# Down projection of a hybrid transformer block: form copies queued one piece later, results finished in the residual's tiles, fewer shared load buffers

## The chip, the cores and the metric

The kernel runs on one NeuronCore of one Trainium2 chip. The metric is the device time of one execution in microseconds; lower is better. The engines named below are TensorE (PE, with its weight loads as PEld), VectorE (DVE), ScalarE (ACT), GpSimd (POOL) and SyncE (SP). Each engine takes its instructions strictly in the order of its own program; SP, ACT and POOL also issue transfers.

## The reference

One transformer block over 256 tokens of width 2048: three kinds of attention merged by gates, an output projection added to the residual, then a gated feed-forward layer with a short causal convolution. Only its last lines matter here:

```python
h2 = rms_norm(x, g_ffn[l])
u = causal_depthwise_conv(h2 @ w_up[l], conv_w[l], conv_b[l])
u_gate, u_val = jnp.split(u, 2, axis=-1)
x = x + (jax.nn.silu(u_gate) * u_val) @ w_down[l]      # 256 x 5632 times 5632 x 2048
```

All tensors are float32. The changed part is the last line, called the down stage here.

## The kernel before, in words

**Number format.** A float32 product is done in three passes. Each operand is split into a rounded part `hi` (type fp32r) and the remainder `lo = x - hi`; `three` (lines 890 to 892) multiplies hi by hi, lo by hi and hi by lo into one PSUM bank. For a weight tile that is loaded into `raw`, `parts` makes `hi` by a cast on ACT (line 885) and `lo` by a subtraction on DVE (line 886). There are four `hi` and four `lo` tiles in rotation, so a cast may start only when PE has read the tile used four casts earlier.

**Pieces.** The 5632 rows of `w_down` are 44 tiles of 128 rows; two neighbours form a piece, 22 pieces in all. The output's 2048 columns are done in two halves (`nb` 0 and 1) of 1024. A piece is multiplied in one of two ways. `eight` is the plain way: eight blocks (two row tiles, two halves of the tokens, two blocks of 512 columns), 24 matmuls in two steps. `seven` does the same with seven products, as Strassen and Winograd do: 21 matmuls in four steps. It needs sums of the weights, two of which (`T`) were made during the stage before and are loaded as `raw_t`; the other two, the plain sums `t13`, are made here by DVE (lines 947 and 948) out of the two loaded tiles `raw_s`. It also needs sums of the activations, the forms. The trace leaves numbers out, so that both `hi_t42` (the split of the loaded `T`) and `hi_t13` (the split of the plain sums) read `hi_t` there.

**Forms.** `forms(p)` prepares piece `p`'s activations: five small DVE instructions (lines 855 to 859) that end in the tile `fr`, then two ACT copies of it to hi parts (lines 862 and 863, into `sf` and `aT`), and then two DVE subtractions for the lo parts (lines 865 and 866). It is a generator: each `yield` ends what is queued in one step, and the rest is queued a step later. There is one `fr` tile.

**Order.** Two strings, `PLANS`, say in which order the pieces come: `s` for seven, `e` for eight. The first half is eeee, eight times se, ee; the second is e, four times se, sse, three times se, ssee. Loads and splits are written two steps ahead of the matmuls that use them. Every instruction of the down stage that is wrapped in `keep` stays on its engine in the order written; PE's matmuls are ordered by the scheduler. A form set is queued with each `e` from the second on, eight sets in the first half and three in the second, so that most of them fall into a repeat of `s` and `e`.

**Load buffers.** `buffer(name)` gives the tiles for loads and for the plain sums: the first six from four tiles tagged `raw`, after that in turn from those and from four tiles tagged `more`. A load waits until its tile has been read by its last reader.

**Results.** `gather` adds the seven-product sums into the residual's tiles `xr`, which POOL loads (line 977). At the end of each half `results` adds the other PSUM banks: DVE writes `o` (line 1016), a tile of the two-tile pool `junk`, and ACT's queue sends it (line 1017). After the first half come one `e` and then the first `s` of the second half, so that these four sends stand in ACT's program ahead of that `s`'s first cast.

Of the kernel before, what the change touches and what calls it, by code (L numbers as in the profile page):

```python
# [9 lines left out]
F32 = mybir.dt.float32  # L10
F32R = mybir.dt.float32r
AF = mybir.ActivationFunctionType
ALU = mybir.AluOpType
AX = mybir.AxisListType

P = 128
# [16 lines left out]
PIECE = 1024  # L33
# [11 lines left out]
def hybrid_block(  # L45
# [25 lines left out]
    nc = tc.nc  # L71
# [5 lines left out]
    sm = ctx.enter_context(tc.tile_pool(name="sm", bufs=4))  # L77
# [742 lines left out]
    def down_pool():  # L820
        if not dn:
            uv.close()
            side.close()
            dn.append(ctx.enter_context(tc.tile_pool(name="dn", bufs=4, side="right", reuse_waits="tile")))
        return dn[0]

    keep = tc.keep_in_program_order
    ov = out[0].rearrange("(t p) d -> p t d", p=P)
# [3 lines left out]
    def pieces_at(p):  # L832
        return aT[:, 2 * p : 2 * p + 2]

    def pieces_of(p):
        return pieces_at(p).rearrange("p k (l t q) -> p k l t q", l=2, t=NT)

    def form_of(p, f):
        if f == FS4:
            return pieces_of(p)[:, 0, :, 1]  # L840
        if p < 10:
            return sf[:, p, f]
        return pieces_at(31 - p).rearrange("p k (f l q) -> p (k f) l q", f=2, l=2)[:, f]

    def forms(p):

        flat = aT[:, 2 * p : 2 * p + 3].rearrange("p k s -> p (k s)").bitcast(F32)
        v = flat[:, :1024].rearrange("p (k l t q) -> p k l t q", k=2, l=2, t=NT)
        d = sm.tile([P, 512], F32, tag="junk", bufs=2, name=f"fd_{p}").rearrange("p (f l q) -> p f l q", f=2, l=2)
        r = down_pool().tile([P, 512], F32, tag="fr", bufs=1, name=f"fr_{p}").rearrange("p (f q) -> p f q", f=4)  # L850
        g = rbc.rearrange("p (k q) -> p k q", k=2)
        two = flat[:, : 2 * 640].rearrange("p (a b) -> p a b", b=640)[:, :, :512]
        two = two.rearrange("p a (l t q) -> p a l t q", l=2, t=NT)[:, :, :, 0]
        tt = nc.vector.tensor_tensor
        keep(tt(d, two, v[:, 0, :, 1].unsqueeze(1).to_broadcast([P, 2, 2, P]), ALU.subtract))
        keep(tt(g, v[:, :, 0, 0], v[:, :, 1, 0], ALU.add))
        keep(tt(r[:, :2], d[:, :, 0], d[:, :, 1], ALU.add))
        keep(nc.vector.scalar_tensor_tensor(r[:, FS2], r[:, FS1], -1.0, g[:, 0], ALU.mult, ALU.subtract))
        keep(tt(r[:, FS4], r[:, FS2], g[:, 1], ALU.add))
        to = sf[:, p] if p < 10 else form_of(p, slice(0, 3))  # L860
        last = form_of(p, FS4)
        keep(nc.scalar.copy(to[:, :, 0], r[:, :3]))
        keep(nc.scalar.copy(last[:, 0], r[:, FS4]))
        yield
        keep(tt(to[:, :, 1], r[:, :3], to[:, :, 0].bitcast(F32), ALU.subtract))
        keep(tt(last[:, 1], r[:, FS4], last[:, 0].bitcast(F32), ALU.subtract))

    turn = [0]

    def buffer(name):  # L870
        turn[0] += 1
        if turn[0] > 6 and turn[0] % 2:
            return down_pool().tile([P, PIECE], F32, tag="more", name=name)
        return wp.tile([P, PIECE], F32, tag="raw", name=name)

    def load(src, name):
        raw = buffer(f"raw_{name}")
        keep(nc.sync.dma_start(raw, src))
        return raw

    def parts(src, name):
        n = src.shape[1]
        hi = wp.tile([P, PIECE], F32R, tag="hi", bufs=SBUFS, name=f"hi_{name}")
        lo = wp.tile([P, PIECE], F32R, tag="lo", bufs=SBUFS, name=f"lo_{name}")
        keep(nc.scalar.copy(hi[:, :n], src))  # L885
        keep(nc.vector.tensor_tensor(lo[:, :n], src, hi[:, :n].bitcast(F32), ALU.subtract))
        return [(hi[:, i : i + 512], lo[:, i : i + 512]) for i in range(0, n, 512)]

    def three(o, ah, al, w, first=False, last=False):
        nc.tensor.matmul(o, lhsT=ah, rhs=w[0], start=first, stop=False)  # L890
        nc.tensor.matmul(o, lhsT=al, rhs=w[0], start=False, stop=False)  # L891
        nc.tensor.matmul(o, lhsT=ah, rhs=w[1], start=False, stop=last)  # L892

    def a_of(k, t):
        a = aT[:, k]
        return a[:, t * P : (t + 1) * P], a[:, S + t * P : S + (t + 1) * P]

    def f_of(p, f):
        to = form_of(p, f)
        return to[:, 0], to[:, 1]  # L900
# [30 lines left out]
    def seven(p, n0, X, Y, first, last):  # L931
        k0, k1 = 2 * p, 2 * p + 1
        name = f"{n0}_{p}"
        w, raw = {}, {}

        def p0():
            raw[0] = load(dv[:, k0, n0 : n0 + PIECE], f"s{n0}_{k0}")
            (w["00"],) = parts(raw[0][:, :512], f"s{n0}_{k0}")

        def p1():  # L940
            raw[1] = load(dv[:, k1, n0 : n0 + PIECE], f"s{n0}_{k1}")
            w["10"], w["11"] = parts(raw[1], f"s{n0}_{k1}")

        def p2():
            raw[2] = load(made[n0 // PIECE, p], f"t{name}")
            raw[3] = buffer(f"t13_{name}")
            keep(nc.vector.tensor_tensor(raw[3][:, :512], raw[0][:, :512], raw[0][:, 512:], ALU.add))
            keep(nc.vector.tensor_tensor(raw[3][:, 512:], raw[0][:, 512:], raw[1][:, 512:], ALU.add))
            w["T4"], w["T2"] = parts(raw[2], f"t42_{name}")

        def p3():
            w["T1"], w["T3"] = parts(raw[3], f"t13_{name}")

        def u0():
            three(Y()[0], *a_of(k0, 0), w["00"], first, last)

        def u1():
            three(X()[0][0], *a_of(k1, 0), w["10"])
            three(X()[0][1], *f_of(p, FS4), w["11"])

        def u2():
            three(Y()[1], *f_of(p, FS2), w["T2"], first, last)
            three(X()[1][0], *a_of(k1, 1), w["T4"])

        def u3():
            three(Y()[2], *f_of(p, FS1), w["T1"], first, last)
            three(Y()[3], *f_of(p, FS3), w["T3"], first, last)

        steps.extend(((p0, u0), (p1, u1), (p2, u2), (p3, u3)))

    xrows = {}
# [25 lines left out]
    banks = {}  # L997
# [9 lines left out]
    def results(nb):  # L1007
        for t in range(NT):
            for n in range(2):
                o = sm.tile([P, 512], F32, tag="junk", bufs=2, name=f"o_{nb}_{t}_{n}")  # L1010
                parts_ = 2 if (nb, t, n) == (1, 1, 1) else 1
                for i in range(parts_):
                    w = 512 // parts_
                    oc = slice(i * w, (i + 1) * w)
                    xc = slice(nb * PIECE + n * 512 + i * w, nb * PIECE + n * 512 + (i + 1) * w)
                    keep(nc.vector.tensor_tensor(o[:, oc], xrows[nb, t, n][:, oc], banks[nb][0][t][n][:, oc], ALU.add))
                    nc.scalar.dma_start(ov[:, t, xc], o[:, oc])

    formed = 0
    after_step = {}  # L1020
# [4 lines left out]
    for nb, plan in enumerate(PLANS):  # L1025
        n0 = nb * PIECE
        ns, s = plan.count("s"), 0
        X, Y = (lambda nb=nb: banks[nb][0]), (lambda nb=nb: banks[nb][1])
        straight = list(range(FT // 2 - 1, ns - 1, -1)) if nb else list(range(ns, FT // 2))
        n_done = 0  # L1030
        at(len(steps) - 1, lambda nb=nb: start(nb))
        for i, c in enumerate(plan):
            if c == "s":
                seven(s, n0, X, Y, s == 0, s == ns - 1)
                s += 1
                if s == ns:
                    at(len(steps) - 1, lambda nb=nb: later(gather(nb, banks[nb][1])))
            else:
                eight(straight.pop(0), n0, X, i == 0, i == len(plan) - 1)
                n_done += 1  # L1040
                if n_done == 4:
                    at(len(steps) - 1, lambda nb=nb: residual(nb))
                if formed < ns and n_done >= 2:
                    at(len(steps) - 2, lambda p=formed: later(forms(p)))
                    formed += 1
        assert s == ns and not straight and formed >= ns
        at(len(steps) - 1, finish)
        at(len(steps) - 1, lambda nb=nb: results(nb))
# [44 lines left out]
```

## Time and profile before

| what | value |
|---|---|
| median of 3 runs | 1517.44 us (1516.77 to 1518.1) |
| the profiled execution: its time, its span | 1517.59 us, 1515.9 us |
| PE, DVE, ACT busy over the span | 98%, 69%, 57% |
| down stage, first to last matmul | 1256.79 to 1509.63 us of the span |

The span is the time from the first to the last instruction seen by the profiler; the execution's own time lies 1.69 us above it. "Busy" PE counts a matmul from its start to its modelled end, and successive matmuls overlap. A row of the timeline has its start, its duration, its engine and line, and in square brackets the idle time before it and what ended that. A row of waits has who waited for whom, the total, the count and the longest. A row of windows has the busy time and the number of instructions of each engine in one stretch, and PE's granted clock.

### The profile page before, as it was taken

The numbers are of one execution on the slowest core, as the hardware profiler recorded it, in microseconds if no ns is written. First come the engines' busy times: TensorE is split into PE (matmuls) and PEld (weight loads), VectorE is DVE, ScalarE is ACT, GpSimd is POOL, SyncE is SP. The second block draws the span as 40 slices with busy tenths as digits, with TensorE's granted clock in tenths as the row PEclk, the third lists the DMA queues.
The fourth block names the chain that finished last, engine by engine and source line by source line (L and its number), as shares of the span: only waits on it lengthen the run. The fifth ranks groups of instructions, "written<-read, shape, count | busy, mean of one in ns | idle before, by whom it ended". The sixth has DMA issues, their size and how long they took to land.

```text
span 1515.9 us, 20136 instructions
## 1 busy us (share of the span) xinstructions
PE 1489.3 (98%) x7408; PEld 1250.9 (83%) x7408; DVE 1044.5 (69%) x1333; ACT 859.6 (57%) x1225; POOL 33.6 (2%) x77
## 2 busy tenths in 40 slices
PE   9999999999999999999999999999999998899998
PEld 7888888888888888888888888888888886677786
DVE  5766566455655556565567877887787776886887
ACT  6755454368444444444566776776676675554553
POOL 0000000001000000000000000000000000000000
PEclk9999999999999999999999999999999999999999
DMA  8675475475667666666677778778777765677784
GB/s 302 193 206 158 128 220 154 126 215 152 197 201 207 191 204 196 191 194 196 210 222 260 254 251 289 237 257 277 250 252 269 250 184 191 208 253 243 226 288 142
DMA packets 156177, 327.70 MB, mean 216 GB/s; under 512 B 11290, under 2 KB 20142, under 8 KB 156078
## 3 DMA queue, kind: packets, MB, share of 16 engines
q1 hardware_dynamic: 150798, 310.15, 66.0%
q0 software_dynamic: 3952, 14.16, 2.6%
q10 hardware_dynamic: 1328, 2.11, 0.4%
q8 instruction: 58, 0.95, 0.3%
q14 instruction: 41, 0.34, 0.1%
HBM read 312.21 MB, written 14.16 MB: 215 GB/s over the span
## 4 chain that ended last, share of the span: by engine, by line
PE 92%; ACT 3%; DVE 2%; issue 1%; DMA 1%; POOL 0%; ACTq 0%; DVEq 0%; SPq 0%; POOLq 0%
PE u L805 22%; PE u L807 11%; PE g L158 5%; PE g L160 5%; PE g L159 5%; PE d L890 4%; PE d L892 4%; PE d L891 4%; PE s L158 2%; PE s L160 2%; PE s L159 2%; PE f L158 2%; PE f L160 2%; PE f L159 2%; PE b L158 2%; PE b L160 2%
## 5 line engine op out<-in xcount | busy, mean ns | idle before, releaser
L805 PE MATMUL u<-hT,hi_u 128*128 128x512 f32 x1408 | 442.4, 396 | 0.1
L807 PEld LDWEIGHTS u<-hT,lo_u 128*128 128x128 f32 x1408 | 264.5, 188 | 62.5
L807 PE MATMUL u<-hT,lo_u 128*128 128x256 f32 x1408 | 276.6, 278 | 0.0
L148 DVE TENSOR_TENSOR lo_u<-raw_u,hi_u 128x1024 fp32r<-128x1024 f32 x176 | 214.2, 1222 | 71.9 <-ACT hi_u L147 70.0
L147 ACT CAST hi_u<-raw_u 128x1024 fp32r<-128x1024 f32 x176 | 183.4, 1048 | 102.0 <-PE u L805 94.4
L805 PEld LDWEIGHTS u<-hT,hi_u 128*128 128x128 f32 x1408 | 214.3, 189 | 0.5 <-issue 0.5
L148 DVE TENSOR_TENSOR lo_g<-raw_g,hi_g 128x1024 fp32r<-128x1024 f32 x96 | 117.7, 1229 | 101.4 <-ACT hi_g L147 98.8
L147 ACT CAST hi_g<-raw_g 128x1024 fp32r<-128x1024 f32 x96 | 100.8, 1052 | 121.8 <-PE g L159 96.9
L158 PE MATMUL g<-hi_g,xT 128*128 128x512 f32 x384 | 150.9, 393 | 0.0
L160 PE MATMUL g<-lo_g,xT 128*128 128x512 f32 x384 | 149.6, 390 | 0.0
L159 PE MATMUL g<-hi_g,xT 128*128 128x512 f32 x384 | 149.5, 389 | 0.0
L160 PEld LDWEIGHTS g<-lo_g,xT 128*128 128x128 f32 x384 | 72.1, 188 | 15.3
L159 PEld LDWEIGHTS g<-hi_g,xT 128*128 128x128 f32 x384 | 72.2, 188 | 14.6
L158 PEld LDWEIGHTS g<-hi_g,xT 128*128 128x128 f32 x384 | 72.1, 188 | 14.5
L890 PE MATMUL d<-hi_d,aT 128*128 128x512 f32 x200 | 79.2, 396 | 4.3 <-ACT hi_d L885 4.3
L744 DVE TENSOR_TENSOR y<-y,z 128x512 f32<-128x512 f32 x88 | 60.8, 691 | 26.9 <-ACT z L743 23.1
L892 PE MATMUL d<-lo_d,aT 128*128 128x512 f32 x200 | 78.7, 394 | 0.0
L891 PE MATMUL d<-hi_d,aT 128*128 128x512 f32 x200 | 78.6, 393 | 0.0
L743 ACT ACTIVATE z<-u,taps 128x256 f32<-128x256 f32 x176 | 74.6, 496 | 0.0
L148 DVE TENSOR_TENSOR lo_s<-raw_s,hi_s 128x1024 fp32r<-128x1024 f32 (+1 forms) x40 | 44.7, 1118 | 37.1 <-ACT hi_s L147 37.1
L148 DVE TENSOR_TENSOR lo_f<-raw_f,hi_f 128x1024 fp32r<-128x1024 f32 (+1 forms) x40 | 44.7, 1119 | 34.5 <-ACT hi_f L147 33.0
L147 ACT CAST hi_f<-raw_f 128x1024 fp32r<-128x1024 f32 (+1 forms) x40 | 38.6, 967 | 52.3 <-PE f L159 47.6
(323 smaller groups left out, 2801.4 us busy)
## 6 DMA issues: line engine op xcount, KB each, us to landing
raw_u<-in_w_up_dram SPq DMA_DIRECT2D x176, 512.0 KB, 4.6
raw_g<-in_w_in_dram SPq DMA_DIRECT2D x96, 512.0 KB, 4.0
raw_d<-in_w_down_dram SPq DMA_DIRECT2D x50, 512.0 KB, 5.6
r<-in_w_down_dram SPq DMA_DIRECT2D x76, 256.0 KB, 5.7
raw_s<-in_w_down_dram SPq DMA_DIRECT2D x38, 512.0 KB, 6.3
raw_f<-in_w_in_dram SPq DMA_DIRECT2D x32, 512.0 KB, 3.7
raw_s<-in_w_in_dram SPq DMA_DIRECT2D x32, 512.0 KB, 3.7
raw_o<-in_w_out_dram SPq DMA_DIRECT2D x32, 512.0 KB, 4.9
```

The source lines that it names most:

```text
L147: pin(nc.scalar.copy(hi[:, :m], raw[:, :m]))
L148: pin(nc.vector.tensor_tensor(lo[:, :m], raw[:, :m], hi[:, :m].bitcast(F32), ALU.subtract))
L158: nc.tensor.matmul(o, lhsT=xh, rhs=wh, start=first, stop=False)
L159: nc.tensor.matmul(o, lhsT=xl, rhs=wh, start=False, stop=False)
L160: nc.tensor.matmul(o, lhsT=xh, rhs=wl, start=False, stop=last)
L743: nc.scalar.activation(z[:, i], u[:, i, j : j + S], AF.Copy, scale=taps_of(j, i))
L744: nc.vector.tensor_tensor(y, y, z, ALU.add)
L805: nc.tensor.matmul(ps, lhsT=hi[:, j, c], rhs=hT[:, k + j, :], start=first, stop=False)
L807: nc.tensor.matmul(ps[:, :S], lhsT=lo[:, j, c], rhs=hT[:, k + j, :S], start=False, stop=last)
L890: nc.tensor.matmul(o, lhsT=ah, rhs=w[0], start=first, stop=False)
L891: nc.tensor.matmul(o, lhsT=al, rhs=w[0], start=False, stop=False)
L892: nc.tensor.matmul(o, lhsT=ah, rhs=w[1], start=False, stop=last)
```

## The change

`forms` gets a second `yield`: the two ACT copies are queued one step after the five DVE instructions, the two subtractions one step after the copies. The plain sums have two tiles of their own (tag `t13`), and loads have six tiles: four `raw` and two `more`, of which every third load takes one. `results` adds in place into `xr` and sends `xr`; the first half's sends go out on POOL's queue, the second's still on ACT's.

```diff
@@ forms
         keep(tt(r[:, FS4], r[:, FS2], g[:, 1], ALU.add))
+        yield
         to = sf[:, p] if p < 10 else form_of(p, slice(0, 3))
@@ buffer
-        if turn[0] > 6 and turn[0] % 2:
-            return down_pool().tile([P, PIECE], F32, tag="more", name=name)
+        if turn[0] > 8 and turn[0] % 3 == 0:
+            return down_pool().tile([P, PIECE], F32, tag="more", bufs=2, name=name)
@@ seven, p2
-            raw[3] = buffer(f"t13_{name}")
+            raw[3] = down_pool().tile([P, PIECE], F32, tag="t13", bufs=2, name=f"t13_{name}")
@@ results
-                o = sm.tile([P, 512], F32, tag="junk", bufs=2, name=f"o_{nb}_{t}_{n}")
...
-                    keep(nc.vector.tensor_tensor(o[:, oc], xrows[nb, t, n][:, oc], banks[nb][0][t][n][:, oc], ALU.add))
-                    nc.scalar.dma_start(ov[:, t, xc], o[:, oc])
+                    xr = xrows[nb, t, n][:, oc]
+                    keep(nc.vector.tensor_tensor(xr, xr, banks[nb][0][t][n][:, oc], ALU.add))
+                    (nc.scalar if nb else nc.gpsimd).dma_start(ov[:, t, xc], xr)
```

The new lines shift the numbers below them by one or two: line 885 of before is 886 after, 1016 is 1017.

ACT's order in one repeat of the first half (the `s` of piece 3). `hi_s_6` and `hi_s_7` are the casts of its two weight tiles, `sf` and `aT` the two form copies, the first `hi_t` is the cast of the loaded sums and the second that of the plain sums. Before:

```order
L885 CAST hi_s_6_11569<-raw_s_6_11567 128x512
L862 CAST sf<-fr_11586 128x3x128
L863 CAST aT<-fr_11586 128x128
L885 CAST hi_s_7_11596<-raw_s_7_11594 128x1024
L885 CAST hi_t_0_3_11619<-raw_t_3_11614 128x1024
L885 CAST hi_t_0_3_11626<-t_0_3_11616 128x1024
```

After:

```order
L886 CAST hi_s_6_11569<-raw_s_6_11567 128x512
L886 CAST hi_s_7_11594<-raw_s_7_11592 128x1024
L863 CAST sf<-fr_11586 128x3x128
L864 CAST aT<-fr_11586 128x128
L886 CAST hi_t_0_3_11617<-raw_t_3_11612 128x1024
L886 CAST hi_t_0_3_11626<-t_0_3_11614 128x1024
```

The second cast of the piece now stands ahead of the two form copies.

DVE's order at the same place, from the last of the five form instructions on. `lo_s_7` needs the cast `hi_s_7`; `t` are the plain sums. Before:

```order
L859 TENSOR_TENSOR fr_11586<-fr_11586,rbc 128x128
L886 TENSOR_TENSOR lo_s_7_11597<-raw_s_7_11594,hi_s_7_11596 128x1024
L865 TENSOR_TENSOR sf<-fr_11586,sf 128x3x128
L866 TENSOR_TENSOR aT<-fr_11586,aT 128x128
L947 TENSOR_TENSOR t_0_3_11616<-raw_s_6_11567 128x512
L948 TENSOR_TENSOR t_0_3_11616<-raw_s_6_11567,raw_s_7_11594 128x512
L886 TENSOR_TENSOR lo_t_0_3_11620<-raw_t_3_11614,hi_t_0_3_11619 128x1024
L886 TENSOR_TENSOR lo_t_0_3_11627<-t_0_3_11616,hi_t_0_3_11626 128x1024
```

After:

```order
L859 TENSOR_TENSOR fr_11586<-fr_11586,rbc 128x128
L887 TENSOR_TENSOR lo_s_7_11595<-raw_s_7_11592,hi_s_7_11594 128x1024
L948 TENSOR_TENSOR t_0_3_11614<-raw_s_6_11567 128x512
L949 TENSOR_TENSOR t_0_3_11614<-raw_s_6_11567,raw_s_7_11592 128x512
L887 TENSOR_TENSOR lo_t_0_3_11618<-raw_t_3_11612,hi_t_0_3_11617 128x1024
L866 TENSOR_TENSOR sf<-fr_11586,sf 128x3x128
L867 TENSOR_TENSOR aT<-fr_11586,aT 128x128
L887 TENSOR_TENSOR lo_t_0_3_11627<-t_0_3_11614,hi_t_0_3_11626 128x1024
```

The two form subtractions moved behind the plain sums and the first `lo_t`. On PE the scheduler answers with the written order in these repeats: a matmul that reads the first `lo_t` now stands ahead of the first one on `hi_t13`, which before came ahead of it.

ACT's order between the halves, before:

```order
L885 CAST hi_d_42_12092<-raw_d_42_12090 128x1024
L885 CAST hi_d_43_12101<-raw_d_43_12099 128x1024
L1017 DMA out_dram<-o_0_0_12129 128x512
L1017 DMA out_dram<-o_0_1_12132 128x512
L1017 DMA out_dram<-o_1_0_12135 128x512
L1017 DMA out_dram<-o_1_1_12138 128x512
L885 CAST hi_s_0_12147<-raw_s_0_12145 128x512
```

On POOL, after, where before the second half's loads of `xr` follow the first half's directly:

```order
L978 DMA xr_1_1_11329<-xkeep_5531 128x512
L1018 DMA out_dram<-xr_0_0_11323 128x512
L1018 DMA out_dram<-xr_0_1_11325 128x512
L1018 DMA out_dram<-xr_1_0_11327 128x512
L1018 DMA out_dram<-xr_1_1_11329 128x512
L978 DMA xr_0_0_12452<-xkeep_5532 128x512
```

The four sends left ACT's program and stand on POOL, ahead of the second half's residual loads.

## The prediction

> **What bounds the kernel now.** I read the chain that ended last first, then PE by stages, then what PE waited for in the down stage, and then one repeat of that stage engine by engine.
>
> ```profile
> PE 92%; ACT 3%; DVE 2%; issue 1%; DMA 1%; POOL 0%; ACTq 0%; DVEq 0%; SPq 0%; POOLq 0%
> ```
>
> PE is the bound, so only time in which PE stands still or runs slowly can be won. The windows of the down stage show where that is (length, then busy time and count of PE, PEld, DVE, ACT, POOL, then PE's granted clock):
>
> ```profile
> 1264.96:1285.64 20.68, 16.35 (x62) 12.73 (x61) 16.01 (x29) 8.73 (x16) 2.19 (x4) 0.83 0.70 226
> 1285.64:1353.00 67.36, 59.50 (x251) 45.55 (x250) 58.28 (x85) 36.85 (x49) 0.00 (x0) 1.00 0.64 208
> 1353.00:1394.29 41.29, 41.29 (x183) 33.98 (x181) 29.98 (x34) 17.31 (x18) 1.64 (x3) 1.00 0.82 276
> 1394.29:1408.74 14.45, 12.52 (x46) 9.46 (x46) 11.28 (x16) 8.06 (x11) 0.55 (x1) 0.88 0.74 217
> 1408.74:1440.00 31.26, 28.16 (x121) 21.84 (x120) 28.16 (x40) 17.22 (x22) 0.00 (x0) 1.00 0.69 215
> ```
>
> The third window is gapless and gives PE's pace: 182 starts in 41.29 us, 0.2269 us for a matmul (one of the 183 began before the window). By it the others lose: 67.36 - 250 x 0.2269 = 10.6 us, 14.45 - 45 x 0.2269 = 4.2 us, 31.26 - 120 x 0.2269 = 4.0 us. The first window, 20.68 - 61 x 0.2269 = 6.8 us, holds the longest wait of this list:
>
> ```profile
> PE d L890 <- ACT hi_t L885: 10.2, 10, 1.2
> PE d L890 <- ACT hi_d L885: 4.3, 1, 4.3
> PE d L890 <- ACT hi_s L885: 2.7, 2, 1.9
> ```
>
> That 4.3 us is for a cast that stands behind the convolution of the stage before on ACT. The change doesn't touch this order, and I leave its 6.8 us where they are. The other two rows are what the change is about.
>
> **Part 1, the form copies.** One repeat on ACT, then DVE, then PE:
>
> ```profile
> 1320.70 0.51 ACT L862 CAST sf<-fr 128x384 fp32r<-128x384 f32 x1 [3.34 <-DVE fr L858]
> 1321.32 1.05 ACT L885 CAST hi_s<-raw_s 128x1024 fp32r<-128x1024 f32 x1
> 1322.27 1.05 ACT L885 CAST hi_t<-raw_t 128x1024 fp32r<-128x1024 f32 x1
> 1325.62 1.04 ACT L885 CAST hi_t<-t 128x1024 fp32r<-128x1024 f32 x1 [2.30 <-PE d L891]
> ```
>
> ```profile
> 1318.99 0.68 DVE L855 TENSOR_TENSOR fd<-aT 128x512 f32<-128x512 f32 x1
> ...
> 1320.70 0.29 DVE L859 TENSOR_TENSOR fr<-fr,rbc 128x128 f32<-128x128 f32 x1
> 1322.40 1.23 DVE L886 TENSOR_TENSOR lo_s<-raw_s,hi_s 128x1024 fp32r<-128x1024 f32 x1 [1.41 <-ACT hi_s L885]
> 1323.55 0.55 DVE L865 TENSOR_TENSOR sf<-fr,sf 128x384 fp32r<-128x384 f32 x1
> 1324.02 0.28 DVE L866 TENSOR_TENSOR aT<-fr,aT 128x128 fp32r<-128x128 f32 x1
> 1324.22 0.68 DVE L947 TENSOR_TENSOR t<-raw_s 128x512 f32<-128x512 f32 x1
> 1324.82 0.68 DVE L948 TENSOR_TENSOR t<-raw_s,raw_s 128x512 f32<-128x512 f32 x1
> 1325.42 1.22 DVE L886 TENSOR_TENSOR lo_t<-raw_t,hi_t 128x1024 fp32r<-128x1024 f32 x1
> 1326.69 1.23 DVE L886 TENSOR_TENSOR lo_t<-t,hi_t 128x1024 fp32r<-128x1024 f32 x1
> ```
>
> ```profile
> 1325.18 0.40 PE L891 MATMUL d<-hi_t,aT 128*128 128x512 f32 x1
> 1326.71 0.50 PE L890 MATMUL d<-hi_t,sf 128*128 128x512 f32 x1 [1.13 <-ACT hi_t L885]
> ...
> 1350.15 0.50 PE L890 MATMUL d<-hi_t,sf 128*128 128x512 f32 x1 [1.13 <-ACT hi_t L885]
> ```
>
> It is a ring. ACT stands 3.34 us at the form copy, which waits for DVE's `fr`. The cast `hi_s` behind it is late, DVE stands 1.41 us for it, and everything behind that on DVE is late: the two form subtractions, the plain sums at 1324.22 and 1324.82, with them the cast of these sums on ACT at 1325.62, and PE. The row names PE as ACT's last releaser there, but the sums ended at 1324.82 + 0.68 = 1325.50, so both held it. The same wait stands at 1350.15, two repeats later: a repeat is (1350.15 - 1326.71)/2 = 11.72 us. It has 21 + 24 matmuls, 45 x 0.2269 = 10.21 us on PE.
>
> With the copies behind `hi_s`, that cast can start when the 512-wide one is done and its buffer is free, before DVE reaches the forms' end. DVE then goes from 1320.99 (1320.70 + 0.29) straight to `lo_s`, 1.41 us earlier. The plain sums also pass the two form subtractions (1323.55 to 1324.22, 0.67 us), so they are ready about 2.1 us earlier, at 1323.4. ACT's cast of the loaded sums now stands behind the form copies (from 1320.70, 0.62 us to the next row), at 1321.3, so ACT is free again at 1322.4. The cast of the plain sums can end about 1324.5; PE was ready for it at 1325.18 + 0.23 = 1325.4, so 0.9 us are in hand. The DVE result that PE wants last, `lo_t` of the plain sums, comes at 1323.4 + 1.2 + 0.7 + 1.2 = 1326.5. In the new matmul order four matmuls stand ahead of its first reader, 1325.4 + 0.9 = 1326.3: 0.2 late, in the frame of this repeat. But DVE enters the repeats late because of stops of the same kind ahead of them, which go too (the first form sets stand between plain pieces there):
>
> ```profile
> DVE lo_d L886 <- ACT hi_d L885: 4.8, 5, 1.5
> ```
>
> So it should enter with more in hand, and what counts is whether it keeps that: DVE works 11.72 - 1.41 = 10.31 us in a repeat by its rows, or 58.28/67.36 x 11.72 = 10.14 us by the window. If the larger figure binds, a repeat lasts 10.31 us and 0.1 us in each of some eight repeats stays, 0.8 us. If the smaller, nothing stays. As these repeats stand between stretches in which DVE has room (29.98 of 41.29 us), I take 0.3 us. PE's new matmul order needs the first `lo_t` sooner, by 1325.0, and it comes at 1323.4 + 1.2 = 1324.6. The form subtractions are late by one step; their readers are PE matmuls of the piece one or more repeats on. Gain: 10.6 + 4.0 - 0.3 = 14.3 us.
>
> **Part 2, the first half's results.** DVE, ACT and PE where the halves meet:
>
> ```profile
> 1386.41 1.28 DVE L1016 TENSOR_TENSOR o<-xr,d 128x512 f32<-128x512 f32 x2
> 1392.44 0.69 DVE L1016 TENSOR_TENSOR o<-xr,d 128x512 f32<-128x512 f32 x1 [4.75 <-DMA out_dram<-o]
> 1394.53 0.69 DVE L1016 TENSOR_TENSOR o<-xr,d 128x512 f32<-128x512 f32 x1 [1.40 <-DMA out_dram<-o]
> ```
>
> ```profile
> 1387.12 8.47 ACTq L1017 DMA_DIRECT2D out_dram<-o  x4
> 1395.71 1.57 ACT L885 CAST hi_s<-raw_s 128x512 fp32r<-128x512 f32 x2 [11.28 <-DVE o L1016]
> ```
>
> ```profile
> 1396.38 0.50 PE L890 MATMUL d<-hi_s,aT 128*128 128x512 f32 x1 [1.93 <-ACT hi_s L885]
> 1397.64 0.63 PE L890 MATMUL d<-hi_s,aT 128*128 128x512 f32 x1
> 1400.47 0.47 PE L890 MATMUL d<-hi_t,sf 128*128 128x512 f32 x1
> ```
>
> DVE's third and fourth add wait for a `junk` tile to be sent; ACT waits at the sends and its casts with it. In place there is no such tile to wait for, and ACT has no send. The adds then wait only for PE's last matmuls of the first half, which end about 24 matmuls (one `e`, 5.4 us) before the `s` at 1394.29, near 1388.9. Cast and subtraction of the first 512-wide piece fit into these 5.4 us (the casts of both its tiles take 1.57 us), so the whole 4.2 us go. Their bounds are 1.9 us (the idle time alone) and 4.2 us; the slow matmuls from 1397.64 to 1400.47 follow at once on the stop, so I take 4.2. [...]
>
> POOL takes over four sends. Behind them it has only the loads of the second half's `xr`, which `gather` reads after that half's last seven-product piece, far behind (1440 is still among its repeats). A send or load that is some microseconds slower is covered by that.
>
> **Part 3, the last results.**
>
> ```profile
> 1506.95 1.28 DVE L1016 TENSOR_TENSOR o<-xr,d 128x512 f32<-128x512 f32 x2
> 1507.67 4.72 ACTq L1017 DMA_DIRECT2D out_dram<-o  x5
> 1510.35 1.46 DVE L1016 TENSOR_TENSOR o<-xr,d 128x512 f32<-128x512 f32 x3 [2.11 <-DMA out_dram<-o]
> ```
>
> The last three adds end at 1511.81, after a wait for a sent tile. Without it the third runs before PE's last matmul ends at 1509.63, and the two half-width ones (1.46 - 0.70 = 0.76 us) follow, to end by 1510.4. The last send leaves 1.4 us earlier. Bounds: 0 if the sends' own time binds, 2.1 if the whole wait goes. I take 1.4.
>
> **Part 4, fewer buffers.** In a repeat five loads and one plain sum went through eight tiles; now five loads go through six. The one load that gets later is the second `raw_s`: it now waits for the plain sums of the repeat before. The rows of loads (KB, median us to landing), and the line of landings over all of them:
>
> ```profile
> raw_s<-in_w_down_dram SPq DMA_DIRECT2D x11, 512.0 KB, 6.2
> raw_t<-T SPq DMA_DIRECT2D x6, 512.0 KB, 3.4
> DMA to landing us min/median/max: 3.4/5.6/8.0
> ```
>
> This makes a loop: sums, load, cast 1.05, subtraction 1.23, sums 1.3, that is landing + 3.6 us for a repeat. At 6.2 us it is 9.8, under PE's 10.21. `raw_t`, which went out first at that moment before, lands in 3.4, and the second `raw_s` now takes its place at the head. So I take zero; the end above is in the rivals.
>
> **Sum.** 14.3 + 4.2 + 1.4 = 19.9 us off the profiled execution's 1517.59 us (span 1515.9, 1.69 around it): 1497.7. The median of the runs, 1517.44, is 0.15 lower: 1497.5 us.
>
> **Rivals.**
> - *Loads come late in part* (12 in 100). Six tiles delay the second `raw_s`; at a landing of 7.0 us the loop is 10.6 us, 0.4 more than PE, in up to 19 pieces done by `seven`: 7.5 us, 1505. For it: landings up to 8.0. Against it: PE's waits name no load, and the median. [...]
> - *Slower*. The same loop from a landing of 7.7 us in all 19 pieces: 11.3 us, 1.1 x 19 = 21 us, which eats the whole gain; at the longest landing seen, 8.0, it is 11.6, 1.4 x 19 = 27 us, 1525. 4 in 100, since the longest would have to be the rule.
> - *DVE becomes the bound* (7). If the late form subtractions push the last `lo_t` behind PE's need by 0.8 us in each of nine repeats, half of part 1 stays: 1505.
> - *The change doesn't do what it says* (4). ACT's cast of the plain sums is released by PE in the rows above, not by DVE; if PE's buffers alone held it, part 1 brings nothing and only 5.6 us are won: 1512. Against it stands DVE's own stop of 1.41 us.
> - *The slow matmuls between the halves stay* (4): only the 1.9 us of idle time go in part 2, and the sum is 2.3 us short, 1499.8. [...]
> - *No difference* (1).
>
> **How the numbers follow.** The forecast itself has 68 in 100, with a range of its own of 1496 to 1500. The range for all reaches from 1495 (both bounds of part 3 and no residue) to 1505, where the first and third rival lie. A measurement of this kernel can tell about 0.2%, 3 us, from no change; all cases but the slower one and the last end below that: faster 0.95, same 0.01, slower 0.04.
>
> **What the next profile would show.** Right: no wait of PE for `hi_t` or `hi_s` left, repeats of 10.2 us, the 4.3 us wait for `hi_d` unchanged; ACT without an 11.28 us stop; DVE's last adds without a wait. Wrong: waits of ACT for `raw_s` loads (rivals one and two), PE waiting for DVE's `lo_t` (rival three), the `hi_t` wait still there (rival four).

## The result and the profile after

The changed kernel takes 1498.12 us, the median of 4 runs (1497.59 to 1498.39); the kernel before took 1517.5 us beside it. The ratio is 0.9872, with an interval of 0.9855 to 0.9889: 1.3% faster. The forecast was 1497.5 us. The profiled execution took 1497.91 us with a span of 1496.2 us, so 19.7 us of span went, where 19.9 were forecast; by the medians it is 19.4 us.

The chain that ended last, and below it all waits of PE from 1250 us to the end (who waited for whom: total, count, longest):

```profile
PE 96%; ACT 2%; DVE 1%; DMA 1%; issue 0%; POOL 0%; SPq 0%; DVEq 0%; POOLq 0%; ACTq 0%
```

```profile
PE d L891 <- ACT hi_d L886: 4.3, 1, 4.3
```

PE's share of the chain rose from 92% to 96%. The rows for `hi_t` (10.2 us) and `hi_s` (2.7 us) are gone; the wait behind the convolution is as it was. The down stage by windows (length, then busy time and count of PE, PEld, DVE, ACT, POOL, then the granted clock):

```profile
1264.44:1285.58 21.14, 16.81 (x61) 13.05 (x61) 19.01 (x33) 11.39 (x19) 1.64 (x3) 0.84 0.61 212
1285.58:1352.00 66.42, 66.42 (x295) 54.99 (x294) 63.49 (x90) 42.17 (x51) 0.00 (x0) 1.00 0.76 262
1352.00:1490.20 138.20, 138.20 (x611) 114.30 (x609) 117.89 (x142) 75.06 (x83) 4.38 (x8) 1.00 0.73 246
```

In the second window PE is busy without a gap, 294 starts in 66.42 us, 0.226 us for one; before, 250 starts took 67.36 us. The third window runs over the meeting of the halves and the whole second half and is gapless too. Only the first still loses: 21.14 - 61 x 0.2269 = 7.3 us.

One repeat, on ACT and then on DVE:

```profile
1320.91 1.05 ACT L886 CAST hi_s<-raw_s 128x1024 fp32r<-128x1024 f32 x1 [0.74 <-PE d L892]
1323.02 0.52 ACT L863 CAST sf<-fr 128x384 fp32r<-128x384 f32 x1 [1.06 <-DVE fr L858]
...
1323.68 1.05 ACT L886 CAST hi_t<-raw_t 128x1024 fp32r<-128x1024 f32 x1
1326.40 1.05 ACT L886 CAST hi_t<-t 128x1024 fp32r<-128x1024 f32 x1 [1.67 <-PE d L892]
```

```profile
1323.02 0.29 DVE L859 TENSOR_TENSOR fr<-fr,rbc 128x128 f32<-128x128 f32 x1
1323.23 1.22 DVE L887 TENSOR_TENSOR lo_s<-raw_s,hi_s 128x1024 fp32r<-128x1024 f32 x1
1324.37 0.68 DVE L948 TENSOR_TENSOR t<-raw_s 128x512 f32<-128x512 f32 x1
1324.97 0.68 DVE L949 TENSOR_TENSOR t<-raw_s,raw_s 128x512 f32<-128x512 f32 x1
...
1327.48 1.23 DVE L887 TENSOR_TENSOR lo_t<-t,hi_t 128x1024 fp32r<-128x1024 f32 x1
```

The cast `hi_s` now starts 2.4 us before `fr` is finished (1323.02 + 0.29), instead of after it. DVE goes from the last form instruction to `lo_s` with no bracket, that is without a wait; its 1.41 us stop is gone. ACT still waits for `fr`, but 1.06 us instead of 3.34, and nothing late stands behind it. The last cast is released by PE alone, 0.75 us after the plain sums' end at 1325.65.

Where the halves meet (DVE's adds, ACT's next cast) and at the end (PE's last matmul, the sends, DVE's adds):

```profile
1375.63 1.28 DVE L1017 TENSOR_TENSOR xr<-xr,d 128x512 f32<-128x512 f32 x2
1377.36 1.74 ACT L886 CAST hi_s<-raw_s 128x512 fp32r<-128x512 f32 x2 [3.71 <-PE d L892]
1378.26 1.29 DVE L1017 TENSOR_TENSOR xr<-xr,d 128x512 f32<-128x512 f32 x2 [1.35 <-PE d L893]
```

```profile
1488.46 4.05 ACTq L1018 DMA_DIRECT2D out_dram<-xr  x5
1490.04 0.39 PE L893 MATMUL d<-lo_d,aT 128*128 128x512 f32 x1
1490.46 1.35 DVE L1017 TENSOR_TENSOR xr<-xr,d 128x512 f32<-128x512 f32 x3 [1.43 <-PE d L893]
```

Between the halves the four adds wait for nothing but PE, and ACT's cast comes 1.7 us after the first add instead of 9.3. At the end the last three adds no longer wait for a send, but now for PE's last matmul. One sign that the prediction had listed as wrong did come, once: ACT waits 1.3 us for a `raw_s` load at 1388.84, and PE does not feel it.

The first matmul of each seven-product piece marks the repeats. Their distances sum up the difference; the ideal is 10.2 us:

| | before | after | gained |
|---|---|---|---|
| 7 repeats of the first half | 13.41, 11.71, 11.67, 11.70, 11.73, 11.71, 10.20 | all 10.20 | 10.7 |
| last of the first half to the first and second of the second | 28.61, 12.36 | 26.52, 10.20 | 4.25 |
| the rest of the second half | 11.33, 11.75, 11.69, then 10.20 and 4.76 | 10.20 and 4.76 | 4.2 |
| start of the down stage to the first piece | 28.85 | 29.31 | -0.5 |
| the stage begins earlier by | | | 0.5 |
| last matmul to the end of the span | 6.66 | 6.16 | 0.5 |

The column adds up to 19.7 us. The two rows of 0.5 cancel, and both look like variation between executions. The fifth row lies ahead of everything that was changed. The fourth holds the 4.3 us wait: in the ten kernels that have this wait, that stretch takes 28.2 to 29.4 us, with the `yield` and without it.

### The profile page after: what moved, and what is told of

It reads as the page before. It is cut to its first block, busy times and chain, and to the rows that moved or that the text cites. A ratio compares the mean times of both kernels' runs of the same rounds, so it can differ in the third digit from the quotient of the medians.

```text
span 1496.2 us, 20140 instructions
## 1 busy us (share of the span) xinstructions
PE 1482.3 (99%) x7408; PEld 1250.7 (84%) x7408; DVE 1043.6 (70%) x1333; ACT 862.9 (58%) x1225; POOL 35.8 (2%) x81
## 3 DMA queue, kind: packets, MB, share of 16 engines
q10 hardware_dynamic: 752, 1.06, 0.2%
## 4 chain that ended last, share of the span: by engine, by line
PE 96%; ACT 2%; DVE 1%; DMA 1%; issue 0%; POOL 0%; SPq 0%; DVEq 0%; POOLq 0%; ACTq 0%
PE u L805 22%; PE u L807 11%; PE g L158 5%; PE g L160 5%; PE g L159 5%; PE d L893 5%; PE d L891 5%; PE d L892 5%; PE s L158 2%; PE s L160 2%; PE f L158 2%; PE f L160 2%; PE s L159 2%; PE f L159 2%; PE b L160 2%; PE b L159 2%
```

## Experiments

All times are medians; the kernel before, run beside them, took 1517.6 us. No kernel leaves work out.

**The parts alone.** First the changed kernel without its new `yield`:

```diff
-        yield
         to = sf[:, p] if p < 10 else form_of(p, slice(0, 3))
```

> The changed kernel without the new yield; results in place and the new buffers stay. Theory (ACT's order of form copies and casts makes the repeated wait of PE): the waits for hi_t come back, some nine of about 1.1 us, and the time is 1498.1 + 14.3 = 1512.4 us. Rival (the buffers or the result path carry that gain too): it stays below 1505 us.

Measured: 1511.28 us (ratio 0.9957, 0.9943 to 0.9972). PE's waits:

```profile
PE d L890 <- ACT hi_t L885: 9.0, 9, 1.2
PE d L890 <- ACT hi_d L885: 4.3, 1, 4.3
```

The `hi_t` wait is back, and the repeats of the first half are 11.7 us again. So the place of the form copies makes that wait, and it is worth 13.2 us on top of the rest; 14.3 were expected. Then the `yield` alone, put into the kernel before:

> The kernel before with the new yield alone. Theory: 1517.5 - 14.3 = 1503.2 us; the waits for hi_t are gone, and between the halves the wait of about 1.9 us for hi_s stays, with slow matmuls right behind it if that stop is what halves the clock. Rival (the late form subtractions need the tiles of their own for the plain sums): some waits for hi_t stay, 1507 us or more.

Measured: 1502.04 us (0.9898, 0.9883 to 0.9913); all repeats of the first half are 10.2 us. What is left is where the halves meet. ACT's and PE's rows there:

```profile
1383.82 1.57 ACT L886 CAST hi_s<-raw_s 128x512 fp32r<-128x512 f32 x2 [10.55 <-DVE o L1017]
1384.49 0.50 PE L891 MATMUL d<-hi_s,aT 128*128 128x512 f32 x1 [1.21 <-ACT hi_s L886]
```

ACT stands 10.55 us at the sends, and PE 1.21 us behind it, where 1.9 us were expected. The clock stays at 1.00 there; the stretch up to the second half's first `s` loses 1.4 us and the one behind it 1.9, 3.3 together, against 4.25 before. The 1.9 us come from DVE, which is late behind the same casts: PE stops twice more, for two low parts.

```profile
1386.70 0.50 PE L893 MATMUL d<-lo_s,aT 128*128 128x512 f32 x1 [0.52 <-DVE lo_s L887]
1389.05 0.50 PE L893 MATMUL d<-lo_t,sf 128*128 128x512 f32 x1 [0.23 <-DVE lo_t L887]
```

Next the results in place alone, put into the kernel before:

```diff
-                o = sm.tile([P, 512], F32, tag="junk", bufs=2, name=f"o_{nb}_{t}_{n}")
...
-                    keep(nc.vector.tensor_tensor(o[:, oc], xrows[nb, t, n][:, oc], banks[nb][0][t][n][:, oc], ALU.add))
-                    nc.scalar.dma_start(ov[:, t, xc], o[:, oc])
+                    xr = xrows[nb, t, n][:, oc]
+                    keep(nc.vector.tensor_tensor(xr, xr, banks[nb][0][t][n][:, oc], ALU.add))
+                    (nc.scalar if nb else nc.gpsimd).dma_start(ov[:, t, xc], xr)
```

> The kernel before with the new result path alone: added in place, the first half sent by POOL. Theory: the 4.2 us between the halves and about 0.5 us at the end (what the changed kernel's trace shows there) go, 1517.5 - 4.7 = 1512.8 us, with no slow matmuls between the halves. Rival (the slow matmuls have another cause): only 1.9 + 0.5 us go, 1515.1 us, and slow matmuls stay near the middle.

Measured: 1511.47 us (0.9959, 0.9944 to 0.9974). The meeting of the halves is at 26.52 and 10.20 us, and the `hi_t` waits stay, 9 of them. It gains 6.1 us, 1.4 more than expected: the two repeats of the second half that follow got shorter too, 10.51 and 11.29 us instead of 11.33 and 11.75. That DVE came into them with less behind is likely, but wasn't tried. So the parts overlap: alone they gain 15.6 and 6.1 us, together 19.4. And this kernel and the one without the `yield`, which differ in the buffers alone, are equal (1511.47, 1511.28). Last the changed kernel with all sends on ACT's queue:

```diff
-                    (nc.scalar if nb else nc.gpsimd).dma_start(ov[:, t, xc], xr)
+                    nc.scalar.dma_start(ov[:, t, xc], xr)
```

> The changed kernel with the first half's sends back on ACT's queue, still in place. Theory (what held ACT was DVE's wait for a tile that was being sent, not the queue): the fourth add ends about 1.3 us after the first half's last matmul, ACT's casts follow within the 5.4 us of the next plain piece, no wait of PE, 1498.1 us. Rival (a send on ACT is what costs): PE waits again between the halves, 1500 us or more.

Measured: 1498.18 us (0.9871, 0.9854 to 0.9887). In the time the queue doesn't show once the adds are in place. The trace is less even: ACT waits for a `raw_s` load in the second half, and the repeat there takes 11.18 us, while the end of the span is 0.4 us shorter.

```profile
1391.70 1.05 ACT L886 CAST hi_s<-raw_s 128x1024 fp32r<-128x1024 f32 x1 [4.26 <-DMA raw_s<-in_w_down_dram]
```

Whether the queue makes that wait, this one trace can't tell. The reverse, results in the two `junk` tiles but the first half's sends on POOL:

```diff
+                o = sm.tile([P, 512], F32, tag="junk", bufs=2, name=f"o_{nb}_{t}_{n}")
...
-                    xr = xrows[nb, t, n][:, oc]
-                    keep(nc.vector.tensor_tensor(xr, xr, banks[nb][0][t][n][:, oc], ALU.add))
-                    (nc.scalar if nb else nc.gpsimd).dma_start(ov[:, t, xc], xr)
+                    keep(nc.vector.tensor_tensor(o[:, oc], xrows[nb, t, n][:, oc], banks[nb][0][t][n][:, oc], ALU.add))
+                    (nc.scalar if nb else nc.gpsimd).dma_start(ov[:, t, xc], o[:, oc])
```

> The changed kernel, but the results are written into the two tiles that were used before the change (the junk tiles) and sent from those; the sends of the first half stay on POOL's queue. Theory (what cost time was that ACT's queue held the sends ahead of its casts, and a send waits for its add): ACT's casts are now free of the sends, and only VectorE can wait, for a junk tile that is still being sent. The third and fourth add wait some 2 to 3 us each with the low parts of the next pieces behind them, so between the halves 0 to 2 us come back: 1498.1 to 1500.5, with the tail 0.5 us longer at most. Rival (the wait for a tile that is being sent is the whole cost, whichever queue sends): the stop between the halves returns in full, 3.4 us as in the kernel with the pinned copies alone: 1501.5 to 1502.0, and the profile shows PE waiting there again.

Measured: 1500.18 us (0.9884, 0.9869 to 0.9899), inside the theory's range. ("The kernel with the pinned copies alone" is the one with the `yield` alone.) DVE's third add and PE a few microseconds on:

```profile
1381.60 1.28 DVE L1017 TENSOR_TENSOR o<-xr,d 128x512 f32<-128x512 f32 x2 [4.69 <-DMA out_dram<-o]
1387.02 0.49 PE L893 MATMUL d<-lo_t,sf 128*128 128x512 f32 x1 [0.68 <-DVE lo_t L887]
```

DVE waits for the sent tile as long as before (4.69 against 4.75 us), but ACT's casts go on and PE is held later and less: the next two repeats lose 1.2 and 0.6 us. Of the 3.9 us from 1502.04 to 1498.12, about half goes with the queue alone; in place, where no add waits for a send, all goes with either queue. So DVE's wait for a sent tile is the root, and sends in ACT's queue about double its price.

**The buffers.** The changed kernel with the eight shared buffers of before:

```diff
-        if turn[0] > 8 and turn[0] % 3 == 0:
+        if turn[0] > 6 and turn[0] % 2:
...
-            raw[3] = down_pool().tile([P, PIECE], F32, tag="t13", bufs=2, name=f"t13_{name}")
+            raw[3] = buffer(f"t13_{name}")
```

> The changed kernel with the buffers of before: eight load buffers in rotation, which the plain sums share, instead of six and two own ones. Theory: loads landed in time with either set, so 1498.1, nothing that can be told from the changed kernel, no new wait of PE. Rival (own tiles for the sums are needed once a repeat takes 10.2 us, because a plain sum then waits for a buffer that a load still holds or the other way round): ACT or PE waits of 0.2 to 1 us in each of the 16 repeats, 1501 to 1514.

Measured: 1498.04 us (0.987, 0.9854 to 0.9887), no new wait. So the buffers' part of the change does nothing to the time that can be told here. How far they may be cut was tried with four load buffers (the `more` tiles never taken) and with five:

> The changed kernel with four load buffers instead of six, the sums' own tiles kept. Theory (a buffer goes round: landing, then the casts and sums that read it; the ring of four is then landing plus 4.8 us per repeat): with landings of 5.2 to 6.2 us a repeat takes 10.0 to 11.0 us instead of 10.2, over 16 repeats 0 to 15 us: 1498 to 1513, and where it is slow, the profile shows casts on ACT that wait for the loads. Rival (depth is of no account, since the engines need only two pieces ahead): 1498.1 and no wait for a load.

> The changed kernel with five load buffers instead of six. With four, a repeat took 12.1 us in the mean, and has five loads; so a buffer went round in four fifths of that, 9.7 us. Theory (what counts is that a buffer's round fits between its turns): with five buffers a turn comes once a repeat, every 10.2 us, over 9.7: no wait, 1498.1 to 1499. Rival (with four the loads were slow as well because they bunched, and the ring that counts runs through the sums of two pieces, so that one buffer fewer than six already delays a load): 10.4 to 11 us a repeat, 1501 to 1511.

Measured: four take 1529.29 us (1.0075, 1.006 to 1.009), slower than the kernel before; five take 1498.43 us (0.9874, 0.9859 to 0.989), with the repeats at 10.2 us. With four, ACT's waits and one turn of the loop (SP's loads, DVE's last plain sum, ACT's casts, DVE's subtractions, the next plain sum):

```profile
ACT hi_d L886 <- DMA raw_d<-in_w_down_dram: 36.1, 20, 3.0
ACT hi_s L886 <- DMA raw_s<-in_w_down_dram: 24.4, 26, 3.1
```

```profile
1316.73 6.03 SPq L879 DMA_DIRECT2D raw_d<-in_w_down_dram  x2
1321.68 0.68 DVE L949 TENSOR_TENSOR t<-raw_s,raw_s 128x512 f32<-128x512 f32 x1
1322.85 1.01 SPq L879 DMA_DIRECT2D raw_s<-in_w_down_dram  x2
1327.20 1.05 ACT L886 CAST hi_d<-raw_d 128x1024 fp32r<-128x1024 f32 x1 [2.73 <-DMA raw_d<-in_w_down_dram]
1328.28 1.23 DVE L887 TENSOR_TENSOR lo_d<-raw_d,hi_d 128x1024 fp32r<-128x1024 f32 x1 [1.84 <-ACT hi_d L886]
1330.19 1.05 ACT L886 CAST hi_s<-raw_s 128x1024 fp32r<-128x1024 f32 x1 [0.62 <-DMA raw_s<-in_w_down_dram]
1332.14 1.22 DVE L887 TENSOR_TENSOR lo_s<-raw_s,hi_s 128x1024 fp32r<-128x1024 f32 x1
1333.87 0.69 DVE L949 TENSOR_TENSOR t<-raw_s,raw_s 128x512 f32<-128x512 f32 x1
```

Depth does count, so the rival of the first falls, but the theory's 1513 was too low by 16 us. The loop is 12.19 us here, and in this turn it runs through `raw_d`. The second `raw_d` goes out right behind the sums (they end at 1322.36, its row at 1322.76), and ACT waits 2.73 us for it; DVE then stands 1.84 us for that cast and works without a wait from 1328.28 to the next sums, the forms' sums among it. 12.19 less this stop is 10.35 us, near PE's 10.2. The second `raw_s`, which the theory had in mind, goes out last of three loads and lands in some 6.5 us, but its cast ends at 1331.24, 0.9 us before DVE comes to the subtraction at 1332.14. The theory had left out the forms on DVE and the load of `raw_d`. One buffer more, the fifth, takes the whole loss away, though ACT then waits ten times for `raw_s`, 1.2 us at most, without PE feeling it. The price of depth here is a step between four and five, and for the time the change kept one buffer more than is needed.

**The wait that is left.** PE's 4.3 us wait and the slow matmuls behind it cost 7.3 us in the window above. ACT has two convolutions ahead of the fourth cast there. They were cut into three parts each, issued one part a piece:

```diff
+    def both(pairs, f0):
+        for i in (0, 2):
+            yield from conv(pairs[i // 2], f0 + i, 1, split=True)
+            if i == 0:
+                yield
...
+            if f0 + 4 == FT and s:
+                later(both(pairs, f0))
```

(`conv` got two `yield`s, after the first activations and after the first sum, and until step 20 only one such generator runs at a time.)

> The changed kernel, with the last two convolutions of the up stage cut into three parts each and issued one part a piece among the first casts of the down stage, instead of both ahead of the fourth cast. Theory: the one wait of PE that is left in the down stage (4.29 us for hi_d, ACT being busy with the convolutions) goes, and with it the half-speed matmuls of some 2.5 us behind it: 1498.1 less 6.8, so 1491.3, with no wait of PE over 0.5 us in the down stage. Rival 1 (the slow matmuls there come from the start of the stage and not from the stop): the 4.3 us go but 2.5 stay, 1493.8. Rival 2 (the forms are now made some 10 us later, and their copies or the interleaved activations hold up the casts): waits of 0.5 to 4 us appear at the first plain pieces, 1495 to 1499.

Measured: 1495.56 us (0.9854, 0.9839 to 0.9869), within rival 2's range. The 4.3 us wait is gone, but PE waits at two other places; not for casts, as rival 2 had it, but for low parts of DVE:

```profile
1285.16 0.50 PE L905 MATMUL d<-lo_d,aT 128*128 128x512 f32 x1 [1.00 <-DVE lo_d L899]
1298.19 0.50 PE L905 MATMUL d<-lo_d,aT 128*128 128x512 f32 x1 [1.76 <-DVE lo_d L899]
```

The forms now begin behind the convolutions, and the sets to be caught up (first sums at 1274.76, 1281.97, 1287.79 and 1294.99 us) left DVE no room beside the low parts. The next two kernels make one set a repeat in the first half, at two different places of the repeat (from the second set on, 5 or 3 in place of the last 6 below):

```diff
-                    at(len(steps) - 2, lambda p=formed: later(forms(p)))
+                    at(len(steps) - 2 if nb else 6 * formed + 6, lambda p=formed: later(forms(p)))
```

> The kernel with the convolutions split, and the forms of the first half also spread: one in each repeat (about 2.9 us of VectorE each, 6.3 us ahead of its first use) instead of three in a row. Theory: VectorE was back to back from 1268.6 to 1300 us in the kernel with the split alone, since three forms had to be made up there, and the two waits of PE for a low part of a straight piece (1.0 and 1.8 us) and the slow start after the second come from that; with 2.9 us less work of VectorE ahead of the second wait that one goes, and with the form behind the two straight pieces' low parts the first as well: 1495.6 less 2.8 less some 1 to 1.4 of slow matmuls: 1491.4 to 1492.0. Rival (VectorE has no room left in a repeat of 10.2 us, so that what is late once stays late): waits of 0.3 to 1 us come at low parts in every repeat, 1496 to 1505.

> The same, but each form one third of a repeat earlier, ahead of the low parts of the two straight pieces, where the kernel with the split had its second form. Theory: only the second wait (1.8 us, and about 1.2 us of slow matmuls behind it) goes, the first of 1.0 us stays: 1492.5 to 1493. Rival as for the other spread kernel: waits of 0.3 to 1 us in every repeat, 1496 to 1505.

Measured: 1496.82 us (0.9862, 0.9845 to 0.988) and 1494.37 us (0.9848, 0.9832 to 0.9864). PE's waits of the one, and of the other:

```profile
PE d L903 <- ACT hi_t L898: 3.8, 7, 0.6
```

```profile
PE d L905 <- DVE lo_d L899: 1.0, 1, 1.0
```

Neither theory held: the first lies within its rival's range, the second between the two. In the first kernel most repeats take 11.1 us: the forms' copies stand ahead of the 1024-wide cast `hi_s` on ACT again, as in the kernel before, DVE stands 0.8 us for that cast, the plain sums are late, and PE waits for the cast of these sums in seven repeats. In the second they take 10.6: the forms' sums stand ahead of the low parts of the straight pieces on DVE, and PE loses 0.4 us in pieces too short to show as waits. So the place in the repeat counts, as in part 1. The last kernel takes the place that the changed kernel has in its steady repeats (the 6 in the line above):

> The kernel with the convolutions split, and each form of the first half made in the very places of a repeat that the changed kernel has (sums behind the low part of the 512-wide plain piece, copies behind the cast of the next piece, low parts ahead of the last low part), but in the repeat that uses it first instead of two repeats earlier. The two other spreads lost 0.4 to 1 us in each repeat, one to a cast that stood behind the forms' copies, one at the low part of a straight piece. Theory (the place within a repeat sets the wait, since VectorE has under half a microsecond to spare in 10.2): the repeats come out at 10.2 us as in the changed kernel, no wait over 0.3 us: 1491.3 to 1492.0. Rival (just ahead is too late: PE needs the form's low part at the second plain piece, before VectorE has made it): a wait of 0.4 to 1 us in each of the eight repeats, 1494 to 1499.

Measured: 1490.99 us, 5 runs of 1490.38 to 1491.69 (0.9825, 0.9812 to 0.9838), with repeats of 10.20 to 10.29 us. No wait of PE is listed in the down stage any more. Its windows, from the place of the old wait on:

```profile
1263.40:1285.00 21.60, 21.60 (x97) 17.86 (x97) 19.75 (x29) 14.47 (x21) 1.63 (x3) 1.00 0.79 269
1285.00:1350.00 65.00, 65.00 (x287) 53.38 (x286) 64.52 (x98) 40.12 (x52) 0.00 (x0) 1.00 0.75 256
```

97 matmuls in 21.60 us, where the changed kernel did 61 in 21.14. The clock is at 1.00 there, so the slow matmuls went with the stop and don't belong to the start of the stage. This version is 7.1 us faster than the changed kernel and 26.6 us faster than the one before.

## Why the prediction was right, and where it was off

- **Part 1 (14.3 us).** The mechanism is shown by the kernels with and without the `yield`. By the distances it gained 10.7 + 4.2 = 14.9 us. The step that was off is the residue of 0.3 us for a DVE that might not keep up: there was none. DVE is busy for 63.49 of the 66.42 us of the gapless window, so it was near to it, and the two misplaced spreads show what happens when something is set at the wrong place there.
- **Part 2 (4.2 us).** Measured 4.25 by the distances, but the right sum hides a term. The forecast added an idle stop of 1.9 us and slow matmuls behind it. In the kernel with the `yield` alone the stop was 1.21 us, the clock stayed at 1.00, and 3.3 us were lost all the same, since PE then waited for DVE's late low parts. So in the kernel before, the slow matmuls probably covered a loss that DVE would have made in good part anyway; no kernel separates the two. Letting them go was right: in the kernel with the results in place alone the distances are 26.52 and 10.20 us, and the rival in which they stay (1499.8) is out. Of the two causes named, DVE's wait for a sent tile is the root: without it nothing is left with either queue. With it, sends in ACT's queue about double the loss.
- **Part 3 (1.4 us).** This is the mis-sized term: 0.5 us. The step that failed is that the third add "runs before PE's last matmul ends". It starts at 1490.46, just behind PE's last matmul (1490.04 + 0.39), though the matmuls of its own 512 columns were done six matmuls earlier. Both 512-column banks of a row tile are one PSUM tile of two banks, and the add seems to wait for the tile's last writer: in ten of the eleven kernels with the results in place the third add starts within 0.04 us of the last matmul's end (with four load buffers DVE comes later). That cause is read from the code and wasn't tried. Beyond it, DVE's adds ended 0.8 us earlier in relation to the last matmul, but the span only 0.5; the rest lies behind the adds, where the last sends are.
- **Part 4 (0).** Right, and shown by the kernels with eight and with five. The loop's margin was less wide than it looked in the repeat above: the second `raw_s` is issued when the sums end, at 1325.7, and its cast stands at 1331.1 (10.2 us after the one at 1320.91), 5.4 us later, against landings of these rows:

```profile
raw_s<-in_w_down_dram SPq DMA_DIRECT2D x38, 512.0 KB, 5.2
raw_t<-T SPq DMA_DIRECT2D x19, 512.0 KB, 5.4
```

  Beyond that a late landing is hidden only because DVE comes to `lo_s` 1.3 us after that cast ends. Over the whole stage `raw_t` went from 4.3 to 5.4 us and `raw_s` from 6.3 to 5.2; with the eight shared buffers they are at 4.4 and 6.4, so the buffers make this difference. The loop itself, landing + 3.6 us, left out the forms on DVE and the loads of `raw_d`, and in the turn of the kernel with four buffers that is shown above, these set it.
- **The sum.** The two terms of 0.5 us that are not the change's cancel. What is left is 14.9 + 4.25 + 0.5 = 19.65 us against 19.9: part 3 gave 0.9 less, and parts 1 and 2 gave 19.15 instead of 18.5. That the sum came so close is in part luck, as these two misses point opposite ways. The lower end of the range doesn't follow from what it names: both bounds of part 3 and no residue give 1497.5 - 0.7 - 0.3 = 1496.5 us, not 1495.
- **The equal gaps.** PE's even gaps went with eight, six and five buffers alike (1498.04, 1498.12 and 1498.43 us), so the number of buffers did not make them. With four left, most repeats are longer, by up to 2.9 us, and ACT's waits name the loads.

## What to carry to other kernels

ACT and DVE ran in the order written here, and what stood behind a waiting instruction came late (ACT's 3.34 us at a form copy, then 1.41 us of DVE and 1.13 us of PE). So when PE's gaps repeat evenly, find the instruction that stands idle longest on the feeding engine and ask whether what stands behind it could go first. DVE has under half a microsecond to spare in a repeat here (busy for 63.49 of 66.42 us), and the same work costs under 0.1 us at one place of the repeat and 0.4 to 0.9 us each time at another; copy the order of a repeat that runs without a gap. DVE's wait for a tile that was still being sent (4.75 us before, 4.69 with the `junk` tiles and POOL's sends) went away when the result was added into the tile that was already there. And before slow matmuls behind a stop are counted as a gain, look at what the feeding engines would have delivered at full speed in that time (with the `yield` alone 3.3 us were lost at a clock of 1.00, of the 4.25 before).

## What the runs showed of the hardware

The clock was halved behind rather short stops, but not behind the shortest. PE's stops in the down stage, over all kernels: of 1.0 to 1.4 us (27 of them, among them the 1.21 us above) none had the clock halved behind it. After the 1.93 us of before and the 1.76 us of the kernel with the split convolutions it was. Windows of before, and then of the split kernel, the first of each holding the stop:

```profile
1393.79:1397.20 3.41, 1.48 (x6) 0.59 (x5) 1.38 (x2) 1.49 (x3) 0.73 (x2) 1.00 0.84 213
1397.20:1400.61 3.41, 3.41 (x8) 2.38 (x9) 3.29 (x4) 1.78 (x3) 0.00 (x0) 0.50 0.30 97
1400.62:1404.03 3.41, 3.41 (x17) 2.78 (x16) 3.35 (x4) 2.71 (x4) 0.00 (x0) 1.00 0.85 251
```

```profile
1295.94:1299.35 3.41, 1.65 (x8) 1.04 (x7) 3.08 (x6) 2.64 (x5) 0.00 (x0) 1.00 0.70 275
1299.35:1302.76 3.41, 3.41 (x10) 2.63 (x9) 3.34 (x10) 0.72 (x2) 0.00 (x0) 0.50 0.84 281
1302.77:1306.18 3.41, 3.41 (x16) 2.79 (x16) 3.41 (x5) 2.33 (x4) 0.00 (x0) 1.00 0.05 17
```

The half clock begins only 0.8 and 1.2 us after PE has started again (1396.38 and 1298.19), lasts 3.41 us both times, and in the split kernel the matmuls in it start 0.43 us apart. After the 4.29 us stop of the ten kernels that have it, 7 to 13 matmuls came 0.4 us or more apart; the half clock lasts 3.41 us in two of them (granted clock over the profiled run: 0.999) and 6.83 in eight (0.996 to 0.998; in the kernel before from 1267.49 to 1274.32 us). What sets the half clock stays open: no stop between 1.42 and 1.76 us was seen, and none was placed on purpose. In the split kernel, where nothing else held PE up, the stop of 1.76 us cost some 1.8 us more than itself: from 1298.19 us on, 44 starts took 11.75 us, where 44 x 0.2269 = 9.98.
